# Context keys and values of the second block: kept in float32, the values computed in two halves at other places

## The chip, the cores and the metric

The kernel is one program on one core of a Trainium2 chip. The time is the device time of one execution in microseconds (us). TensorE (PE) multiplies, its weight loads are listed apart (PEld); VectorE is DVE, ScalarE is ACT, GpSimd is POOL, and SyncE (SP) issues nearly all transfers of weights from memory (HBM).

## The reference, cut to what matters

Two transformer blocks run one after the other on 256 tokens of width 1024. The first ends in a mixture of 32 experts; the second is a hybrid of a long convolution and an attention that also looks at a context of 256 tokens.

```python
# end of block one: each token goes to two of 32 experts
hb = jax.nn.silu(xb @ w1[e]) * (xb @ w3[e]);  out = hb @ w2[e]     # w1, w3: 1024x512, w2: 512x1024
x = rmsnorm(x + y, norm_f_g)
# block two: keys and values of the context do not depend on x
hc = modulate(rmsnorm_2(ctx, g_mix_pre), csh1, csc1)               # 256 x 1024
kv_c = hc @ w_in[:, OFF_K:OFF_G]                                   # 512 keys, 512 values; 1024 deep
h = modulate(rmsnorm_2(x, g_mix_pre), sh1, sc1);  proj = h @ w_in
k_all = concat([k, k_c]);  v_all = concat([v, v_c])                # used by the attention, late
```

## The kernel before, in words

All weights come through one queue, SP's, in tiles of 1 MB (128 partitions x 2048 float32). A ring of buffers (`wtile`, `wload`) gives each load the next slot, and SP issues a load when the slot's last reader is done; SP works in order, so a load whose slot is held stops those behind it.

A dense product in front of and behind the experts is exact to about float32 by splitting: each weight row block is split by ACT (`wh`, line 298) and DVE (`wl`, line 299) into a high and a low part of type fp32r, the other operand is split too (`cxh`, `cxl` for the context), and PE makes three products: high x high, low x high, high x low (`dense`, lines 310 to 312; `dense_T`, lines 346 to 348). The experts' products are single float32 products, read straight from the loaded tile (lines 1268 and 1298).

The stage that matters runs like this. After the cross attention of block one, x is transposed (line 268), scores for groups and experts are made (`lg`, line 852), and DVE finds each token's two experts in a chain of small operations that ends in `ea`; PE counts with it (`pp`, lines 906 to 910), DVE makes the one-hot rows (`hot`), and PE gathers the tokens of the first four experts (`pxg`, line 938). The context's keys (`ctx_k`, into `kTc`) and values (`ctx_v`, into `vc`) are written behind this in the code; the scheduler that builds the program places instructions of one engine by when their inputs are expected, so that they stand between the steps of the router.

Then come 16 cycles j of two experts each. A cycle is w1 (`up`, eight loads of 1 MB with w3), w2 of the cycle before (`down`, four loads), w3, the combination of the cycle before (`py`, line 1016), a gather for a later pair, in cycles 7 to 14 a piece of the second block's filters (`hooks`: `f1` to `fH`), and a transposition (`turn`). Two experts share PE, 64 columns each. The ring has 14 slots (4 `wpA`, 10 `wpB`); `change_ring` in `ctx_v` adds the two `xTB` buffers, which `cxh` and `cxl` held until then. In cycle 6 (`filters`) the ten `wpB` slots go and two `wpC` come, in cycle 15 (`wide_ring`) three more.

Behind the last combination stands a norm: ACT and DVE sum squares (`norm_part`), POOL takes the power, x is scaled (`xs`), PE transposes it (line 268), and ACT and DVE split it into `x2h` and `x2l`, into the same two `xTB` buffers, for the first products of block two.

Of the kernel before, what the change touches and what calls it, by code (L numbers as in the profile page):

```python
# [8 lines left out]
F32 = mybir.dt.float32  # L9
# [3 lines left out]
AF = mybir.ActivationFunctionType  # L13
# [4 lines left out]
P = 128  # L18
D = 1024
S = 256  # L20
# [81 lines left out]
def _body(nc, tc, I, out, ctx, dbg):  # L102
    V, A, G, T = nc.vector, nc.scalar, nc.gpsimd, nc.tensor

    traced = []
# [13 lines left out]
    def acc(name="acc"):  # L119
        return ps.tile([P, 512], F32, name=name, tag="acc", bufs=4)  # L120
# [7 lines left out]
    def xTt(name, g="A", dt=F32R, shape=(P, 8, S)):  # L128
        return wk.tile(list(shape), dt, name=name, tag="xT" + g, bufs=2)
# [4 lines left out]
    def tap(name, ap):  # L134
        if name in dbg:
            nc.gpsimd.dma_start(dbg[name], ap)
# [8 lines left out]
    def change_ring(new, gone=()):  # L145

        i = ring["i"] % len(ring["slots"])
        set_ring([pl for pl in ring["slots"][i:] + ring["slots"][:i] if pl not in gone] + new)
# [16 lines left out]
    def wloads(wsrc, c0, n, KB=8):  # L165
        return [wload(wsrc[kb * P:(kb + min(4, KB - kb)) * P, c0:c0 + n], min(4, KB - kb), n) for kb in range(0, KB, 4)]
# [104 lines left out]
    def tr_split(src, KB, gcol=None, sc=1.0, bcol=None, hl=None, name="t", g="A"):  # L271

        hi, lo = hl if hl else (xTt(name + "h", g), xTt(name + "l", g))
        for kk in range(0, KB, 2):
            pv = tr4(src, kk)
            if gcol is None:
                hilo(hi[:, kk:kk + 2, :], lo[:, kk:kk + 2, :], pv, sc)
                continue
            for j in range(2):
                k = kk + j  # L280
                if bcol is None:
                    hilo(hi[:, k, :], lo[:, k, :], pv[:, j, :], gcol[:, k:k + 1])
                else:
                    last["hi"] = A.activation(hi[:, k, :], pv[:, j, :], AF.Identity, bias=bcol[:, k:k + 1],  # L284
                                              scale=gcol[:, k:k + 1])
                    lo_of(lo[:, k, :], hi[:, k, :], pv[:, j, :], gcol[:, k:k + 1], bcol[:, k:k + 1])
        return hi, lo
# [14 lines left out]
    def dense(xh, xl, KB, ws, n, consume, ahead=None, tail=0):  # L302


        accs = [acc(), acc()]

        def products(k, t, h, l):
            s = slice(t * P, (t + 1) * P)
            p = accs[t][:, :n]
            T.matmul(p, xh[:, k, s], h[:, :n], start=k == 0, stop=False)  # L310
            T.matmul(p, xh[:, k, s], l[:, :n], start=False, stop=False)  # L311
            T.matmul(p, xl[:, k, s], h[:, :n], start=False, stop=k == KB - 1)  # L312
        held = []
        for k in range(KB):
            if ahead:
                ahead(k)
            held.append((k, split(ws[k // 4][:, k % 4, :], n)))
            if pend:
                pend.pop(0)()
            if k < KB - tail:  # L320
                for t in range(2):
                    products(k, t, *held[-1][1])
                held.pop()
            if k % 4 == 3 and after:
                after.pop(0)()
        for t in range(2):
            for k, hl in held:
                products(k, t, *hl)
            consume(t, accs[t][:, :n])

    def dense_T(xh, xl, KB, ws, n, consume, ahead=None):


        nb = n // P
        accs = [acc().rearrange("p (b s) -> p b s", b=2) for _ in range(0, nb, 2)]
        for k in range(KB):
            if ahead:
                ahead(k)
            h, l = split(ws[k // 4][:, k % 4, :], n)
            if pend:  # L340
                pend.pop(0)()
            for b in range(nb):
                s = slice(b * P, (b + 1) * P)
                p = accs[b // 2][:, b % 2, :]

                T.matmul(p, h[:, s], xh[:, k, :], start=k == 0 and b % 2 == 0, stop=False)  # L346
                T.matmul(p, h[:, s], xl[:, k, :], start=False, stop=False)  # L347
                T.matmul(p, l[:, s], xh[:, k, :], start=False, stop=k == KB - 1 and b in (nb - 1, b // 2 * 2 + 1))  # L348
            if k % 4 == 3 and after:
                after.pop(0)()  # L350
        for i, p in enumerate(accs):
            consume(i, p[:, :min(2, nb - 2 * i), :])
# [42 lines left out]
    def copy_to(dst, **kw):  # L395
        def c(t, p):
            A.activation(dst[:, t, :], p, AF.Copy, **{k: v[:, t:t + 1] for k, v in kw.items()})
        return c
# [277 lines left out]
    for g in range(8):  # L676
        p = smp("pmix")
# [121 lines left out]
    softmax(0)  # L799
    softmax(1)  # L800
    wxo = [wloads(I["w_xo"][0], ch * 512, 512) for ch in range(2)]
    wck = [wloads(I["w_in_2"][0], 2048 + ch * 512, 512) for ch in range(2)]
    for ch in range(2, 4):
        dense(mh, ml_, 8, W["w_xkv", ch], 512, copy_to(vx[:, :, (ch - 2) * 512:(ch - 1) * 512], scale=rm))
    oh, ol = xTt("oh", "A"), xTt("ol", "A")
# [11 lines left out]
    rc = rsq(sumsq(cx), 2, 1.0 / D)  # L817
    for t in range(2):
        V.tensor_scalar(cx[:, t, :], cx[:, t, :], rc[:, t:t + 1], None, op0=OP.mult)
    ch_, cl_ = tr_split(cx, 8, mods[:, 1, :], bcol=mods[:, 6, :], name="cx", g="B")  # L820
    for ch in range(2):
        dense(oh, ol, 8, wxo[ch], 512, add_x(ch))
    tap("x2", x)
# [129 lines left out]
    V.tensor_copy(pre_, p[:, :96].rearrange("p (c n) -> p c n", c=3))  # L953


    def ctx_k():
        def c_kc(i_, p):
            A.activation(kTc[:, 2 * i_:2 * i_ + 2, :], p, AF.Copy)
        dense_T(ch_, cl_, 8, wck[0], 512, c_kc)

    def ctx_v():
        dense(ch_, cl_, 8, wck[1], 512, copy_to(vc))
        change_ring(["xTB"] * 2)
    ctx_k()
    ctx_v()


    ge = mo.tile([P, 2, 4], F32, name="ge")
# [147 lines left out]
    def lambdas():  # L1116
        V.tensor_tensor(lv[:, 0:2, :], lv[:, 0:2, :], lv[:, 2:4, :], op=OP.mult)
        ls = mo.tile([1, 2], F32, name="ls")
        V.tensor_reduce(ls, lv[:, 0:2, :], AX.X, OP.add)
        A.activation(ls, ls, AF.Exp)  # L1120
        V.scalar_tensor_tensor(ls[:, 0:1], ls[:, 0:1], 0.2, ls[:, 1:2], op0=OP.add, op1=OP.subtract)
        p = smp("lam")
        traced[:] = [T.matmul(p[:, 0:1], ones[0:1, :], ls[:, 0:1], start=True, stop=True)]
        V.tensor_copy(lam, p[:, 0:1])
# [151 lines left out]
    def turn(sg):  # L1276
        p = tpp()
        for q in range(4):
            traced[:] = [T.transpose(p[:, q * P:(q + 1) * P], sg[:, q * P:(q + 1) * P], ident)]
        hT = wk.tile([P, 4, P], F32, name="hT", tag="wl", bufs=4)  # L1280
        A.activation(hT, p.rearrange("p (q s) -> p q s", q=4), AF.Copy)  # L1281
        return hT
# [19 lines left out]
    def gather_some(n):  # L1302
        for _ in range(min(n, len(todo))):
            todo.pop(0)()
# [14 lines left out]
    def after_down(j, po, done=None):  # L1319
        with pe_after():  # L1320
            combine(rows[:, 0], slotc[:, j:j + 1], po, done)
    for j in range(NJ):
        if j == 2:
            with pe_after():
                po = down(1, hT)
            with pe_after():
                gather_some(2)
            after_down(1, po)
            hT = None
            traced.clear()  # L1330
            overflow(n_over)
            traced.clear()
        if j % 2 == 0 and j + 2 < NJ:
            xg_, st_ = group(j + 2)
            xgs[j + 2] = xgs[j + 3] = xg_
            todo += st_
        h1 = acc("hw1")
        with pe_after():
            up(j, "w1", h1, (0, 1))
        sg = act_half(h1)  # L1340
        if j in (6, 15):
            hooks[j]()
        po = None
        if hT is not None:
            with pe_after():
                po = down(j - 1, hT)
        h3 = acc("hw3")
        with pe_after():
            up(j, "w3", h3, (0, 1))
        V.tensor_tensor(by_row(sg, 4), by_row(sg, 4), in_block(h3, 4), op=OP.mult)  # L1350
        if j == 0:
            lambdas()
            n_over = nc.values_load(novi[0:1, 0:1], min_val=0, max_val=7)
            with pe_after():
                bc_rows(rows[:, 0], dest)
                bc_rows(rows[:, 1], gt)
        if po is not None:
            after_down(j - 1, po)
        with pe_after():
            gather_some(4)  # L1360
        if 6 < j < 15 and j in hooks:
            with pe_after():
                hooks[j]()
        with pe_after():
            hT = turn(sg)
    with pe_after():
        po = down(NJ - 1, hT)
    after_down(NJ - 1, po, norm_part)
    tap("x3", x)
    moctx.close()  # L1370

# [18 lines left out]
    with tc.issue_after(last["hi"].ins):  # L1390
        for t in range(2):
            A.activation(x[:, t, :], xr[:, t, :], AF.Copy, scale=r1[:, t:t + 1])
    tap("xp", x)
    late["wc"].close()
    set_ring([wpA] * NA)
# [293 lines left out]
```

## Time and profile before

| | |
|---|---|
| median of 3 runs | 1294.23 us (1293.45 to 1294.81) |
| profiled execution | 1296.29 us, span 1294.6 us |
| PE busy | 1240.6 us (96%) |
| DVE, ACT, POOL busy | 747.9, 552.5, 70.2 us |
| read from HBM | 363.00 MB, 281 GB/s over the span |
| first and last expert product begin (line 1268) | 388.43 us, 838 us |

The page cuts the span into 40 slices of 32.4 us; slices 13 to 26 are the experts. Matmul rows are records: a float32 product appears as two, an fp32r product as one; their ends are modelled, and successive ones overlap, so the distance of two starts is the cost of one.

### The profile page before, as it was taken

What the parts mean: (1) busy time and instruction counts of PE and PEld (TensorE: products, weight loads), DVE (VectorE), ACT (ScalarE), POOL (GpSimd) and SP (SyncE); (2) the same over time, 40 slices, a digit from 0 to 9 for tenths busy, and PEclk for the clock granted to TensorE, in tenths of its full rate; (3) what the DMA queues carried; (4) which work ended last, traced back from release to release, by engine and by line L of the source; (5) the groups of instructions that cost most, each with busy time, mean ns of one, the idle gap of its engine ahead of it and who ended that gap; (6) DMA issues with size and microseconds to landing.
All of it is one profiled execution on the core that took longest, in us unless ns stands there. A gap on an engine that the chain in (4) does not pass through costs nothing.

```text
span 1294.6 us, 18193 instructions
## 1 busy us (share of the span) xinstructions
PE 1240.6 (96%) x6920; PEld 897.6 (69%) x6920; DVE 747.9 (58%) x1474; ACT 552.5 (43%) x1016; POOL 70.2 (5%) x118
## 2 busy tenths in 40 slices
PE   7999999999999999989899999979999998999996
PEld 7987788998884444433344444449878996799985
DVE  5996888746761413213341332369897787566654
ACT  6867455746551111111111111156255556445542
POOL 1101100100000000100000000010000101000000
PEclk9999999999999999999999999979999999999999
DMA  9764774994439999999999999967362666565751
GB/s 348 259 210 157 267 238 155 391 383 155 155 125 405 419 419 421 403 420 420 421 405 403 421 421 414 417 260 255 117 207 103 232 159 250 189 226 171 240 180 48
DMA packets 103243, 365.29 MB, mean 282 GB/s; under 512 B 6840, under 2 KB 9203, under 8 KB 78960
## 3 DMA queue, kind: packets, MB, share of 16 engines
q1 hardware_dynamic: 93264, 329.77, 67.6%
q0 software_dynamic: 9744, 34.18, 7.6%
q8 instruction: 56, 0.92, 0.3%
q14 instruction: 35, 0.29, 0.1%
q10 hardware_dynamic: 144, 0.14, 0.1%
HBM read 363.00 MB, written 1.06 MB: 281 GB/s over the span
## 4 chain that ended last, share of the span: by engine, by line
PE 50%; DMA 9%; issue 3%; DVE 2%; ACT 1%; POOL 1%; SPq 0%; DVEq 0%; POOLq 0%; ACTq 0%
PE hw L1268 13%; DMA w<-in_w_dram 7%; PE acc L347 5%; PE acc L346 5%; PE acc L348 5%; PE po L1298 3%; PE acc L312 2%; PE acc L311 2%; PE acc L310 2%; PE py L1016 2%; PE pxg L938 1%; PE iy L1454 1%; PE fH L1207 1%; PE s L1496 1%; DMA w<-in_w_ffn_gate_dram 1%
## 5 line engine op out<-in xcount | busy, mean ns | idle before, releaser
L298 ACT ACTIVATE wh<-w 128x512 fp32r<-128x512 f32 (+1 forms) x454 | 278.8, 622 | 242.7 <-PE acc L312 105.4
L299 DVE TENSOR_TENSOR wl<-w,wh 128x512 fp32r<-128x512 f32 (+1 forms) x454 | 303.5, 683 | 134.1 <-ACT wh L298 131.6
L1268 PE MATMUL hw<-w,xg 128*64 128x512 f32 x1024 | 234.8, 595 | 14.8 <-DMA w<-in_w_dram 12.9
L1268 PEld LDWEIGHTS hw<-w,xg 128*64 128x64 f32 x1024 | 79.3, 137 | 154.6 <-issue 127.2
L240 DVE SCALAR_TENSOR_TENSOR otl<-po,gs,oth 128x512 fp32r<-128x512 f32 x32 | 24.0, 749 | 208.7 <-ACT oth L239 207.9
L1298 PE MATMUL po<-w,hT 128*64 128x512 f32 x512 | 120.0, 595 | 2.2 <-ACT hT L1281 1.5
L1298 PEld LDWEIGHTS po<-w,hT 128*64 128x64 f32 x512 | 44.4, 137 | 72.1 <-issue 63.6
L939 ACT ACTIVATE xg<-pxg,vec 128x256 f32<-128x256 f32 x64 | 29.6, 476 | 139.3 <-PE pxg L938 139.0
L347 PE MATMUL acc<-xfl,wh 128*128 128x256 f32 x288 | 82.1, 285 | 0.0
L346 PE MATMUL acc<-xfh,wh 128*128 128x256 f32 x288 | 82.1, 285 | 0.0
L348 PE MATMUL acc<-xfh,wl 128*128 128x256 f32 x288 | 82.0, 285 | 0.0
L452 DVE SCALAR_TENSOR_TENSOR junk<-waT,cb 128x1024 bf16<-128x1024 f32 x64 | 78.1, 1220 | 3.6 <-DMA waT<-in_l_waT_dram 3.2
L311 PE MATMUL acc<-wl,xmh 128*128 128x512 f32 x192 | 76.7, 399 | 0.8 <-DVE wl L299 0.7
L312 PE MATMUL acc<-wh,xml 128*128 128x512 f32 x192 | 76.3, 398 | 0.0
L310 PE MATMUL acc<-wh,xmh 128*128 128x512 f32 x192 | 75.9, 399 | 0.0
L1350 DVE TENSOR_TENSOR sg<-sg,hw 128x512 f32<-128x512 f32 x16 | 11.0, 689 | 106.5 <-PE hw L1268 106.5
L239 ACT ACTIVATE oth<-po,gs 128x512 fp32r<-128x512 f32 x32 | 22.0, 687 | 101.2 <-PE po L1298 101.0
L347 PE MATMUL acc<-x2l,wh 128*128 128x256 f32 x224 | 64.3, 289 | 0.5 <-DVE x2l L246 0.5
L346 PE MATMUL acc<-x2h,wh 128*128 128x256 f32 x224 | 64.3, 292 | 0.3 <-ACT x2h L284 0.3
L348 PE MATMUL acc<-x2h,wl 128*128 128x256 f32 x224 | 64.4, 289 | 0.0
L347 PEld LDWEIGHTS acc<-xfl,wh 128*128 128x128 f32 x288 | 54.8, 190 | 0.0
L348 PEld LDWEIGHTS acc<-xfh,wl 128*128 128x128 f32 x288 | 54.8, 190 | 0.0
(542 smaller groups left out, 2568.8 us busy)
## 6 DMA issues: line engine op xcount, KB each, us to landing
w<-in_w_dram SPq DMA_DIRECT2D x188, 1024.0 KB, 13.6
w<-in_w_in_dram SPq DMA_DIRECT2D x54, 1024.0 KB, 6.3
waT<-in_l_waT_dram POOLq DMA_DIRECT2D x48, 512.0 KB, 5.3
w<-in_w_ffn_gate_dram SPq DMA_DIRECT2D x10, 1024.0 KB, 5.3
w<-in_w_ffn_up_dram SPq DMA_DIRECT2D x10, 1024.0 KB, 5.3
w<-in_w_ffn_down_dram SPq DMA_DIRECT2D x10, 1024.0 KB, 5.3
w<-in_w_out_dram SPq DMA_DIRECT2D x8, 1024.0 KB, 5.4
w<-in_w_xkv_dram SPq DMA_DIRECT2D x8, 1024.0 KB, 14.2
```

What stands on the lines that cost most here:

```text
L298: last["act"] = A.activation(h[:, :n], w, AF.Copy)
L299: last["dve"] = V.tensor_tensor(l[:, :n], w, f(h[:, :n]), op=OP.subtract)
L310: T.matmul(p, xh[:, k, s], h[:, :n], start=k == 0, stop=False)
L311: T.matmul(p, xh[:, k, s], l[:, :n], start=False, stop=False)
L312: T.matmul(p, xl[:, k, s], h[:, :n], start=False, stop=k == KB - 1)
L346: T.matmul(p, h[:, s], xh[:, k, :], start=k == 0 and b % 2 == 0, stop=False)
L347: T.matmul(p, h[:, s], xl[:, k, :], start=False, stop=False)
L348: T.matmul(p, l[:, s], xh[:, k, :], start=False, stop=k == KB - 1 and b in (nb - 1, b // 2 * 2 + 1))
L452: V.scalar_tensor_tensor(junk(), w[i_][:, b, :], 1.0, cb[:, r_, :], op0=OP.mult, op1=OP.mult, accum_out=adac[:, n, r_:r_ + 1])
L939: A.activation(xg[:, k, :], p, AF.Copy, scale=col["l_gmoe"][:, k:k + 1])
L1268: traced[:] = [T.matmul(hps[64 * e:64 * e + 64, :], xgs[j][:, 4 * kb + k, s0 + 64 * e:s0 + 64 * e + 64], we[e][:, k, :], start=kb + k == 0 ...
L1298: traced[:] = [T.matmul(po[hf][64 * e:64 * e + 64, :], hT[:, 2 * kb + q, 64 * e:64 * e + 64], we[e][:, q, hf * 512:(hf + 1) * 512], start= ...
```

## The change

The context stays in float32: transposed once (`cxT`), modulated by ACT, not split. Its keys are single float32 products, eight deep steps for four blocks of 128 keys, read from the unsplit weights. The values are made in two halves of 256 columns: the first half is loaded behind the weights of the first cycle and multiplied behind that cycle's gathers; the second half is loaded ahead of the last experts' w2 and multiplied behind the last combination. `cxT` takes one of the two `xTB` buffers until then, so the ring gets one, not two; the value weights are two loads of 1 MB in rows of 1 KB (before, two of 1 MB in rows of 2 KB, ahead of the experts).

```diff
-    wck = [wloads(I["w_in_2"][0], 2048 + ch * 512, 512) for ch in range(2)]
+    wck = wloads(I["w_in_2"][0], 2048, 512)
...
-    ch_, cl_ = tr_split(cx, 8, mods[:, 1, :], bcol=mods[:, 6, :], name="cx", g="B")
+    cxT = xTt("cxT", "B", F32)
+    for kk in range(0, 8, 2):
+        pv = tr4(cx, kk)
+        for j in range(2):
+            k = kk + j
+            A.activation(cxT[:, k, :], pv[:, j, :], AF.Identity, bias=mods[:, 6, k:k + 1], scale=mods[:, 1, k:k + 1])
+    change_ring(["xTB"])
...
-    def ctx_k():
-        def c_kc(i_, p):
-            A.activation(kTc[:, 2 * i_:2 * i_ + 2, :], p, AF.Copy)
-        dense_T(ch_, cl_, 8, wck[0], 512, c_kc)
-    def ctx_v():
-        dense(ch_, cl_, 8, wck[1], 512, copy_to(vc))
-        change_ring(["xTB"] * 2)
-    ctx_k()
-    ctx_v()
+    kc = [acc("kc") for _ in range(2)]
+    for k in range(8):
+        for b in range(4):
+            T.matmul(kc[b // 2][:, b % 2 * S:(b % 2 + 1) * S], wck[k // 4][:, k % 4, b * P:(b + 1) * P], cxT[:, k, :],
+                     start=k == 0 and b % 2 == 0, stop=k == 7 and b % 2 == 1)
+    for i_ in range(2):
+        A.activation(kTc[:, 2 * i_:2 * i_ + 2, :], kc[i_].rearrange("p (b s) -> p b s", b=2), AF.Copy)
+    def ctx_v(wv):
+        pv = [acc("cv")[:, :256] for _ in range(2)]
+        for k in range(8):
+            for t in range(2):
+                traced[:] = [T.matmul(pv[t], cxT[:, k, t * P:(t + 1) * P], wv[:, k, :], start=k == 0, stop=k == 7)]
+        return pv
+    def ctx_v_load(hf):
+        return wload(I["w_in_2"][0][:, 2560 + 256 * hf:2560 + 256 * (hf + 1)], 8, 256)
+    def ctx_v_out(hf, pv):
+        for t in range(2):
+            A.activation(vc[:, t, 256 * hf:256 * (hf + 1)], pv[t], AF.Copy)
...
             lambdas()
+            wv = ctx_v_load(0)
...
             gather_some(4)
+        if j == 0:
+            with pe_after():
+                ctx_v_out(0, ctx_v(wv))
...
+    wv = ctx_v_load(1)
     with pe_after():
         po = down(NJ - 1, hT)
     after_down(NJ - 1, po, norm_part)
+    with pe_after():
+        pv = ctx_v(wv)
...
             A.activation(x[:, t, :], xr[:, t, :], AF.Copy, scale=r1[:, t:t + 1])
+        ctx_v_out(1, pv)
```

On PE at the end of the router, before: the last products of the keys and values (`acc`), around the counts `pp`.

```order
L348 MATMUL acc<-cxh,wl 128x256
L310 MATMUL acc<-wh,cxh 128x512
L311 MATMUL acc<-wl,cxh 128x512
L312 MATMUL acc<-wh,cxl 128x512
L906 MATMUL pp<-ea,rt__3677 128x32
L907 MATMUL pp<-ea,rt__3677 128x32
L908 MATMUL pp<-ea,ca 128x32
L909 MATMUL pp<-ea,ca 128x32
L910 MATMUL pp<-ea,ca 128x32
L310 MATMUL acc<-wh,cxh 128x512
```

The same place after the change, from the last scores (`lg`) to the first gather; `kc` are the float32 keys.

```order
L858 MATMUL lg<-rt__3648,xmT 128x36 x9
L965 MATMUL kc<-cxT,w 128x256 x9
L912 MATMUL pp<-ea,rt__3648 128x32
L913 MATMUL pp<-ea,rt__3648 128x32
L914 MATMUL pp<-ea,ca 128x32
L915 MATMUL pp<-ea,ca 128x32
L916 MATMUL pp<-ea,ca 128x32
L965 MATMUL kc<-cxT,w 128x256 x7
L944 MATMUL pxg<-hot,xnh 128x256
```

Nine key products now stand ahead of `pp` and seven behind it; another seven stand behind the gathers, and the values are gone from here.

On SP's queue from the weights of the context to the first expert loads, before (`novi` is a number that SP reads to decide on a branch):

```order
L162 DMA w<-in_w_in_dram 128x4x512 x4
L1233 DMA w<-in_w_dram 128x2048 x13
L1353 TENSOR_LOAD novi
L1353 ISA x2
L1233 DMA w<-in_w_dram 128x2048 x19
```

And after:

```order
L162 DMA w<-in_w_in_dram 128x4x512 x2
L1251 DMA w<-in_w_dram 128x2048 x8
L162 DMA w<-in_w_in_dram 128x8x256
L1251 DMA w<-in_w_dram 128x2048 x5
L1372 TENSOR_LOAD novi
L1372 ISA x2
L1251 DMA w<-in_w_dram 128x2048 x20
```

The first half of the values (128x8x256) stands among the first expert loads; ahead of `novi` there are 13 expert loads in both.

On PE behind the last combination (`py`), after the change; before, the transposes `tp` followed `py` at once.

```order
L1034 MATMUL py<-oth,ET 128x512 x4
L1034 MATMUL py<-otl,ET 128x512 x4
L975 MATMUL cv<-w,cxT 128x256 x16
L268 MATMUL tp<-ca,xs_6783 128x128 x8
```

The 16 value products stand between the combination and the transposes.

## Rows read from the trace of the kernel before

**Rows 1.** The page's slices of 32.4 us: bytes moved.

```profile
GB/s 348 259 210 157 267 238 155 391 383 155 155 125 405 419 419 421 403 420 420 421 405 403 421 421 414 417 260 255 117 207 103 232 159 250 189 226 171 240 180 48
```

**Rows 2.** Stretches of the expert stage: us, busy (records) by engine, PEclk, DMA share, GB/s.

```profile
core 0: us, PE busy (x) PEld busy (x) DVE busy (x) ACT busy (x) POOL busy (x), PEclk, DMA share, GB/s
...
583.00:598.00 15.00, 11.83 (x53) 5.00 (x50) 4.02 (x7) 1.38 (x2) 0.00 (x0) 1.00 1.01 419
...
688.00:703.00 15.00, 15.00 (x80) 8.85 (x81) 2.96 (x5) 3.59 (x7) 0.00 (x0) 1.00 0.97 391
763.00:778.00 15.00, 14.72 (x66) 5.81 (x63) 3.12 (x9) 1.97 (x3) 0.00 (x0) 1.00 1.01 421
```

**Rows 3.** PE's timeline in the expert stage: start, us, what, [idle before, releaser].

```profile
388.43 13.95 PE L1268 MATMUL hw<-w,xg 128*64 128x512 f32 x64
...
407.10 7.09 PE L1268 MATMUL hw<-w,xg 128*64 128x512 f32 x32
...
551.54 2.79 PE L1298 MATMUL po<-w,hT 128*64 128x512 f32 x10 [0.60 <-DMA w<-in_w_dram]
...
774.59 3.65 PE L1268 MATMUL hw<-w,xg 128*64 128x512 f32 x14 [0.28 <-DMA w<-in_w_dram]
```

**Rows 4.** Groups by line: one of the keys' three product groups, busy, mean ns.

```profile
L346 PE MATMUL acc<-cxh,wh 128*128 128x256 f32 x32 | 9.4, 293 | 0.0
```

**Rows 5.** PE's timeline: float32 products, then fp32r products of keys and of values.

```profile
322.79 7.07 PE L810 MATMUL po<-pT,vx 128*128 128x256 f32 x32
...
369.90 0.28 PE L346 MATMUL acc<-cxh,wh 128*128 128x256 f32 x1
370.02 0.28 PE L347 MATMUL acc<-cxl,wh 128*128 128x256 f32 x1
...
386.07 0.39 PE L312 MATMUL acc<-wh,cxl 128*128 128x512 f32 x1
386.30 0.39 PE L310 MATMUL acc<-wh,cxh 128*128 128x512 f32 x1
```

**Rows 6.** Timelines of DVE and PE through the router.

```profile
365.37 0.42 DVE L867 SCALAR_TENSOR_TENSOR lg<-lg,rxm,brt 128x36 f32<-128x36 f32 x2
...
366.49 0.70 DVE L299 TENSOR_TENSOR wl<-w,wh 128x512 fp32r<-128x512 f32 x1
...
372.61 0.23 DVE L904 TENSOR_TENSOR ea<-E 128x64 f32<-128x64 f32 x1
...
372.89 0.41 PE L906 MATMUL pp<-ea,rt__3677 128*128 128x32 f32 x2
```

**Rows 7.** SP's timeline: issues of expert loads, start of the first, until the last.

```profile
384.62 4.55 SPq L1233 DMA_DIRECT2D w<-in_w_dram  x3
...
392.11 7.67 SPq L1233 DMA_DIRECT2D w<-in_w_dram  x6
...
682.84 5.30 SPq L1233 DMA_DIRECT2D w<-in_w_dram  x3
...
701.02 4.24 SPq L1233 DMA_DIRECT2D w<-in_w_dram  x4
```

**Rows 8.** Loads by line, 280 to 480 us, then the last w2 loads.

```profile
DMA to landing us min/median/max: 5.0/12.5/19.9
...
L1294 SPq DMA_DIRECT2D w<-in_w_dram x8: 328/328/422, 824.2 to 834.9; - x8
...
DMA to landing us min/median/max: 11.5/13.3/15.5
```

**Rows 9.** PE's timeline at the end of the experts.

```profile
842.75 7.09 PE L1298 MATMUL po<-w,hT 128*64 128x512 f32 x32 [0.75 <-ACT hT L1281]
...
859.93 1.99 PE L268 MATMUL tp<-ca,xs 128*128 128x128 f32 x8 [7.65 <-DVE xs L1387]
```

**Rows 10.** Stretches around the norm, columns as in rows 2.

```profile
844.00:848.00 4.00, 4.00 (x22) 1.33 (x20) 0.00 (x0) 0.00 (x0) 0.00 (x0) 1.00 1.04 389
...
864.00:868.00 4.00, 4.00 (x21) 4.00 (x21) 3.24 (x7) 2.69 (x6) 0.00 (x0) 0.50 1.01 398
...
872.00:880.00 8.00, 8.00 (x68) 7.99 (x68) 6.56 (x15) 5.86 (x9) 0.53 (x1) 1.00 0.52 195
```

## The prediction

> **What bounds the kernel now.** I read the bytes per slice first: slices 13 to 26 take some 400 to 421 GB/s, the ones around them far less [rows 1]. That is the expert stage, 32 experts of 6 MB each, all through SP's queue. Then the stage in stretches of 15 us: at 583:598 the DMA share is 1.01 at 419 GB/s while PE is busy for 11.83 of 15 us; at 763:778 PE has 14.72 and the DMA is still at 1.01 [rows 2]. PE's timeline says how it gets there. It starts the experts at 388.43 with its slots full, so for six cycles it runs at its own pace; the first wait on a load ends at 551.54, and the last, of 0.28 us, at 774.59 [rows 3]. So the stream of loads sets the middle of the stage, and PE and stream are level at its end. What counts is therefore not when PE starts the experts but when the stream starts, how much it still has to bring, and whether it ever runs out of free slots. At 421 GB/s a load of 1 MB takes 2.5 us.
>
> **1. The context products ahead of the experts (gain).** Removed on PE: 96 products of 256 columns for the keys (three groups of 32) [rows 4] and, by the same code, 3 x 16 of 512 columns for the values. Start to start they take 0.12 and 0.23 us [rows 5]: 96 x 0.12 + 48 x 0.23 = 22.5 us. Added there: the keys alone, 8 x 4 float32 products of 256 columns. The 16 products of that shape at line 810 are 32 records in 7.07 us with the tail of the last [rows 5], 0.43 us a product from start to start; 32 x 0.43 = 13.8 us. Net -8.7 us.
>
> What it loses is cover. In the new order nine key products stand between the router's scores and the counts (pp), seven between these and the gathers. DVE takes up the scores at 365.37 and begins ea, which pp waits for, at 372.61; between them stand seven splits wl like the one at 366.49, which push the next step back by 0.6 us each [rows 6]. They go: 4.2 us. On ACT one norm of x now stands ahead of two xmT copies, which I put at 0.5 us later scores. So pp can start at 372.89 - 4.2 + 0.5 = 369.2; PE, with nine products of 0.43 us behind the score products, which end when DVE takes them up (365.9), is there at 369.8. Behind pp the one-hot rows lose two splits and come at about 374.2, PE's seven products end at 374.0. With a wait for the first xmT copies I take 1.1 us of waits in all; the bounds are 0 and 4.2 us (no split's time comes back). **The experts start at 388.43 - 8.7 + 1.1 = 380.8**, 7.6 us earlier.
>
> **2. The stream of loads (takes most of it back).** Before, 13 loads are there and three more are issued from 384.62 to 389.2: the 14th, and two into the xTB buffers, freed when the context values end; pairs follow from 392.11 [rows 7]. A load into an empty queue lands 5.0 us after issue [rows 8], 2.5 of it transfer. So the 15th starts at about 388.8 + 2.5 = 391.3, load k lands at 391.3 + 2.5(k - 14), the 24th at 416.3.
>
> After, the ring has one xTB buffer (the other holds cxT to the end of the stage), and one of its 15 slots holds the first half of the value weights. At 380.8 there are again 13 expert loads, and the 14th is issued then, into the slot of the second key weights; it lands at 385.8. The next slots come back in pairs from 380.8 + 3.7 = 384.5 on (3.7 as from 388.43 to 392.11), four pairs until w3 ends at 380.8 + 14.0 = 394.8 [rows 3]. The first of them starts at 387, and the 22nd load has landed by 407. Before, PE was back at weights 4.7 us after the end of w3 (402.4 to 407.10). Now 16 value products stand there as well, 16 x 0.43 = 6.9 us: the value slot is free at about 405.9 and the first pair behind it at 410. The 23rd load lands at 410.9, the 24th at 415. The queue runs empty for 1.4 and 1.6 us. **The stream is 1.3 us ahead of before, not 7.6**: two loads fewer in store (5.0 us) and the gaps. PE itself is 7.6 - 6.9 = 0.7 us ahead and meets the stream where it did.
>
> **3. One slot fewer until the end (loses).** From the seventh cycle on the ring has 8 slots before and 7 after. The longest stretch without a release runs from the last issue of the three at 682.84 (688.1) to 701.02, 12.9 us [rows 7]. The pair ahead of it was in use for 4.0 us, and a new load needs 2.5 us to start: what is queued must last 19.4 us. 8 x 2.5 = 20 us does, 7 x 2.5 = 17.5 us falls 1.9 us short. Even with eight, that stretch has a share of 0.97 [rows 2]. Six cycles carry hooks of this kind, half of them as long as this one: 3 x 1.9 = 5.7 us at most, and 0 if loads that PE has not reached cover the gaps. I take 1.0, nearer to none, because PE waits little there [rows 3].
>
> **4. The second value load.** It stands in SP's queue ahead of the last eight half loads of w2. Those are issued until 834.9 and the last lands at least 11.5 us later, at 846.4 [rows 8]; PE needs it for the last quarter of the 7.09 us from 842.75, at 848.1 [rows 9]: a slack of 1.7 us. Where rows of 2 KB and 4 KB share the queue, it moves 389 GB/s [rows 10], and 1 MB takes 2.7 us; rows of 1 KB are in no row of a full queue, so 2.7 is the nearest. 2.7 - 1.7 = 1.0; the bounds are 0 (the stream has gained on PE by then) and 2.7.
> [...]
>
> **Expert stage: -1.3 + 1.0 + 1.0 = +0.7 us.**
>
> **5. The second half under the norm (free).** PE idles for 7.65 us ahead of the transposes at 859.93 [rows 9]; 6.9 us fit with 0.7 to spare, and the two copies out of PSUM stand on ACT behind the last split of x2. If that cover is gone, what exceeds it is paid in full.
>
> **6. The clock (gain).** [...]
>
> **Sum.** +0.7 - 1.5 = -0.8 us on the profiled execution's 1296.29 us, 1295.5. That execution took 2.1 us more than the median of the runs, so the median comes to 1294.2 - 0.8 = **1293.4 us**. The splits that go on ACT and DVE lie beside a full PE and bring nothing of their own.
>
> **Rivals.**
> - *The lead is kept* (28%). The queue does not run empty in the first cycle and w2 is not late: -4.3 for step 2, 0 for steps 3 and 4, -2.5 for the clock: 1294.2 - 6.8 = 1287.4. For it: PE waits for no load before 551. Against: every slot behind the value products comes back 6.9 us late.
> - *Seven slots starve the stream* (22%), slower. Step 3 in full, the clock at -1.0: -1.3 + 5.7 + 1.0 - 1.0 = +4.4, 1298.6. It decides where a stretch without a release passes 17.5 - 4.0 - 2.5 = 11.0 us. For it: the 0.97 with eight slots. Against: PE and stream are level there, so part of a gap is never waited for.
> - *The router's wait takes the products' place* (8%): waits of 4.2 rather than 1.1 us shift the stream by 3.1: 1296.5.
>
> **How the numbers follow.** The forecast has 42%, its own range is 1291.5 to 1295.5. No change means within 0.2%, 2.6 us, about what a measurement of this kernel can tell. Faster: nearly all of the first rival and a little of the forecast, 0.31. Slower: most of the second, half of the third, a little of the forecast, 0.26. Same: 0.43. A range that leaves out 2 in 10 goes from 1287.5 to 1298.5.
>
> **What would show it.** The first expert product near 381, not 388 us (step 1; later than 383 is the third rival). GB/s that dip between 404 and 413 us, and a first wait on a load within 3 us of before's (step 2; no dip is the first rival). DMA shares under 0.97 where the hooks are long (step 3). PE busy from the last py to the transposes, and a granted clock of 1.00 behind them (steps 5 and 6). The prediction is wrong if the last combination ends more than 3 us earlier or later than before.

## The result, and the profile after

The changed kernel took 1303.88 us (median of 4 runs, 1303.70 to 1305.19) against 1294.49 us (4 runs): a ratio of 1.0079, 95% interval 1.0064 to 1.0094. It is 9.4 us slower, and 1303.88 lies outside the predicted range, 1287.5 to 1298.5. Its profiled execution took 1303.7 us, span 1302.0 us.

The page's bytes per slice, to be laid beside [rows 1]:

```profile
GB/s 345 256 209 164 257 246 154 392 372 162 174 123 381 372 413 420 410 399 420 422 398 390 411 409 387 404 311 254 172 178 115 199 200 216 208 225 187 239 178 48
```

The stream loses mainly at three places: 381 for 405 in the 13th slice (391 to 423 us here), with the value half of the first cycle; 372 for 419 in the 14th, with the branch around the overflow code; and 398, 390, 411, 409, 387 and 404 in the 21st to 26th, the last third of the experts, where [rows 1] has 405, 403, 421, 421, 414 and 417.

PE's timeline (start, us, what, [idle before, releaser]), to be laid beside [rows 3] and [rows 9]:

```profile
380.74 13.95 PE L1286 MATMUL hw<-w,xg 128*64 128x512 f32 x64
398.87 7.07 PE L975 MATMUL cv<-w,cxT 128*128 128x256 f32 x32
...
448.31 16.46 PE L1286 MATMUL hw<-w,xg 128*64 128x512 f32 x64 [6.20 <-PEq L1049]
...
565.25 5.34 PE L1286 MATMUL hw<-w,xg 128*64 128x512 f32 x14 [3.26 <-DMA w<-in_w_dram]
...
815.02 3.65 PE L1286 MATMUL hw<-w,xg 128*64 128x512 f32 x14 [1.43 <-DMA w<-in_w_dram]
...
853.56 7.39 PE L1316 MATMUL po<-w,hT 128*64 128x512 f32 x32 [0.75 <-ACT hT L1299]
861.51 1.31 PE L1034 MATMUL py<-oth,ET 128*128 128x512 f32 x4 [0.56 <-ACT oth L239]
863.58 7.07 PE L975 MATMUL cv<-w,cxT 128*128 128x256 f32 x32
871.53 1.22 PE L268 MATMUL tp<-ca,xs 128*128 128x128 f32 x8 [0.88 <-DVE xs L1413]
873.35 0.50 PE L346 MATMUL acc<-x2h,wh 128*128 128x256 f32 x2 [0.60 <-ACT x2h L284]
...
880.60 0.63 PE L268 MATMUL tp<-ca,xs 128*128 128x128 f32 x4 [1.13 <-DVE tb L245]
```

The experts start 7.7 us earlier than before, and the last w2 product starts 10.8 us later (853.56 for 842.75). The first loss is in plain sight: PE idles for 6.20 us in front of cycle 2, and its sequencer (PEq) at line 1049, the branch around the overflow code, is named as the releaser. Waits for loads go on to 815.02, where before the last, of 0.28 us, was at 774.59.

Line 1049 of the changed kernel and the same line of the kernel before (1031): durations in ns (min/median/max), start in us. SP, ACT and DVE pass in 45 to 72 ns in both; PE does not:

```profile
L1049 SPq COMPARE_BRANCH  x1: 50/50/50, 424.6 to 424.6; - x1
L1049 ACTq COMPARE_BRANCH  x1: 45/45/45, 440.4 to 440.4; - x1
L1049 PEldq COMPARE_BRANCH  x1: 6065/6065/6065, 441.9 to 441.9; - x1
L1049 DVEq COMPARE_BRANCH  x1: 72/72/72, 442.8 to 442.8; - x1
```

```profile
L1031 PEldq COMPARE_BRANCH  x1: 445/445/445, 442.7 to 442.7; - x1
```

The transfers fit a wait for instructions. Queue 8 carries instructions, 55 packets and 0.90 MB in the whole execution, which is 16 KB for every 251 of the 13,808 records of PE and PEld: it follows PE. From 20 to 434 us of the kernel before, 18 packets move beside 4613 records, 256 a packet. The last of these packets ahead of the branch's end moves at 434 to 436 us before, some 7 us ahead of the branch, and at 444 to 446 us after, behind the branch's start (before first; packets, MB, share):

```profile
q8 instruction: 1, 0.02, 3.4%
```

```profile
q8 instruction: 1, 0.02, 3.5%
```

Windows of the changed kernel (us, busy and records by engine, PEclk, DMA share, GB/s) show what the stall sets off: behind it PE runs in part at a granted clock of 0.50 (448 to 452 us; the 64 records take 16.46 for 13.95 us), its slots come back late, and the stream has a hole, 146 GB/s at 450 to 455.

```profile
450.00:455.00 5.00, 5.00 (x18) 1.67 (x16) 1.90 (x7) 0.00 (x0) 0.00 (x0) 0.66 0.37 146
690.00:840.00 150.00, 145.49 (x668) 67.99 (x666) 37.08 (x74) 24.52 (x44) 0.00 (x0) 1.00 0.98 400
```

The second row, to be laid beside this one of the kernel before, is the other loss: 15 GB/s over 150 us are 2.25 MB or 5.3 us of the stream.

```profile
690.00:840.00 150.00, 149.43 (x697) 70.37 (x696) 39.05 (x81) 25.89 (x46) 0.54 (x1) 1.00 1.01 415
```

### The profile page after: what moved, and what is told of

Its sections match the earlier page's. It is cut to its first block, busy times and chain, and to the rows that moved or that the text cites. A ratio compares the mean times of both kernels' runs of the same rounds, so it can differ in the third digit from the quotient of the medians.

```text
span 1302.0 us, 18103 instructions
## 1 busy us (share of the span) xinstructions
PE 1244.6 (96%) x6904; PEld 897.2 (69%) x6904; DVE 731.9 (56%) x1442; ACT 542.6 (42%) x1002; POOL 70.0 (5%) x118
## 3 DMA queue, kind: packets, MB, share of 16 engines
HBM read 363.00 MB, written 1.06 MB: 280 GB/s over the span
## 4 chain that ended last, share of the span: by engine, by line
PE 52%; DMA 8%; DVE 2%; ACT 2%; issue 1%; POOL 0%; DVEq 0%; POOLq 0%; ACTq 0%
PE hw L1286 13%; DMA w<-in_w_dram 7%; PE acc L347 5%; PE acc L346 5%; PE acc L348 5%; PE po L1316 5%; PE acc L312 2%; PE acc L310 2%; PE acc L311 2%; PE py L1034 2%; PE pxg L944 1%; PE iy L1481 1%; PE fH L1225 1%; PE s L1523 1%; DMA w<-in_w_ffn_gate_dram 1%
## 5 line engine op out<-in xcount | busy, mean ns | idle before, releaser
L299 DVE TENSOR_TENSOR wl<-w,wh 128x512 fp32r<-128x512 f32 (+1 forms) x438 | 292.4, 682 | 134.9 <-ACT wh L298 133.9
L298 ACT ACTIVATE wh<-w 128x512 fp32r<-128x512 f32 (+1 forms) x438 | 268.9, 622 | 230.1 <-PE acc L312 102.3
L1286 PE MATMUL hw<-w,xg 128*64 128x512 f32 x1024 | 241.5, 604 | 23.2 <-DMA w<-in_w_dram 17.0
L1316 PE MATMUL po<-w,hT 128*64 128x512 f32 x512 | 116.2, 594 | 1.5 <-ACT hT L1299 1.5
```

The costliest lines, as they stand in the source:

```text
L298: last["act"] = A.activation(h[:, :n], w, AF.Copy)
L299: last["dve"] = V.tensor_tensor(l[:, :n], w, f(h[:, :n]), op=OP.subtract)
L1286: traced[:] = [T.matmul(hps[64 * e:64 * e + 64, :], xgs[j][:, 4 * kb + k, s0 + 64 * e:s0 + 64 * e + 64], we[e][:, k, :], start=kb + k == 0 ...
L1316: traced[:] = [T.matmul(po[hf][64 * e:64 * e + 64, :], hT[:, 2 * kb + q, 64 * e:64 * e + 64], we[e][:, q, hf * 512:(hf + 1) * 512], start= ...
```

## The experiments

Two theories on the branch. P: the code behind it lies in a block of instructions that was not yet fetched when PE arrived. Q: SP, whose queue has one more load in front of the same branch, is late, and all engines meet there. Two on the waits after 690. S: seven slots are too few. L: the stream was merely late from the hole on. "Last w2" is the start of the last w2 products, the clearest mark of the stage's end; GB/s is the window 690 to 840.

| run | time, us | against before, 95% interval | branch, ns | last w2 | slots | GB/s |
|---|---|---|---|---|---|---|
| before | 1294.49 | | 445 | 842.75 | 8 | 415 |
| changed | 1303.88 | 1.0064 to 1.0094 | 6065 | 853.56 | 7 | 400 |
| e1 page moved | 1300.53 | 1.0040 to 1.0086 | 445 | 847.61 | 7 | 395 |
| e2 page, before | 1296.54 | 1.0011 to 1.0038 | 6225 | 846.06 | 8 | 417 |
| e3 seven slots | 1301.16 | 1.0042 to 1.0081 | 458 | 852.70 | 7 | 390 |
| e4 half in cycle 7 | 1297.80 | 1.0027 to 1.0057 | 445 | 846.77 | 7 | 399 |
| c1 early, slot back | 1293.51 | 0.9993 to 1.0018 | 445 | 843.28 | 8 | 416 |
| c2 early, seven | 1297.74 | 1.0024 to 1.0059 | 442 | 849.07 | 7 | 404 |
| c3 key half late | 1299.37 | 1.0039 to 1.0077 | 445 | 848.84 | 8 | 416 |
| d1 later start | 1299.01 | 1.0029 to 1.0057 | 458 | 850.29 | 8 | 413 |
| c4 shrink +1 | 1293.42 | 0.9990 to 1.0013 | 445 | 843.68 | 8 | 417 |
| c5 shrink +2 | 1298.45 | 1.0026 to 1.0060 | 445 | 848.62 | 8 | 405 |
| f1 changed again | 1302.54 | 1.0059 to 1.0093 | 5926 | 852.08 | 7 | 399 |
| f2 e1 again | 1300.53 | 1.0041 to 1.0078 | 445 | 849.30 | 7 | 393 |

The kernel before ran beside each group, at medians of 1293.1 to 1294.3. The marks and windows come from one trace for each run: the two traces of the changed kernel (f1 is the second) differ by 1.5 us at the last w2 product, those of e1 and f2, one kernel too, by 1.7.

**e1, e2: the branch moved within its block.** The edit puts tiny products ahead of all of PE's work, in its first wait of 7.4 us: 24 in the changed kernel, 41 in the kernel before.

```diff
     G.memset(nhalf, -0.5)
+    pad = tpp("pad")
+    for _ in range(24):
+        T.matmul(pad[0:8, 0:8], nhalf, nhalf, start=True, stop=True)
```

> The changed kernel with 24 products of 8x8 (a few columns each) ahead of everything on TensorE, in its first wait of 7.4 us; nothing else moves, but each TensorE instruction after them stands 96 places later, so that the branch around the overflow code stands 3 places behind where the kernel before has it, and not 93 ahead of it. Theory P (the branch's target lies in a page of instructions that was not yet fetched; the 6.07 us of the branch on TensorE are that fetch): the branch takes under 1 us (0.445 before), the first w1 product of cycle 2 starts at 442 to 445 (448.31 in the changed kernel), the clock stays full there, the loads have no hole at 450 to 457. Rival Q (SyncE reaches the branch late, since one more load stands ahead of it and one slot is gone, and all engines meet there): the branch still takes 6 us and the time stays at 1303.9. What P is worth in the end tells two further theories apart. S (seven slots): the four waits for loads at 720 to 815 stay (4.4 us), 1297 to 1300. L (the stream was only late from the hole on): they go too, 1292.5 to 1295.5.

> The kernel before with 41 such products ahead of everything on TensorE: its branch now stands where the changed kernel's does within a block of 256 instructions. Theory P: the branch takes 4 to 7 us (0.445), 1298.5 to 1301.5. Rival Q: the branch is not touched, 1294.5 within 0.7.

The branch on PE, e1 first, then e2:

```profile
L1052 PEldq COMPARE_BRANCH  x1: 445/445/445, 440.6 to 440.6; - x1
```

```profile
L1034 PEldq COMPARE_BRANCH  x1: 6225/6225/6225, 443.0 to 443.0; - x1
```

P holds both ways and Q falls: the stall leaves the changed kernel and appears in the kernel before, with SP's queue untouched. The packet of queue 8 goes the same way: in e1 it moves at 432 to 434 us, ahead of the branch, in e2 at 446 to 448, behind the branch's start. In e1 the first w1 product of cycle 2 starts at 442.64, the granted clock of 372 to 520 is 1.00 (0.98 in the changed kernel), and the first wait for a load ends at 551.94, where [rows 3] has 551.54. Of the time, less than expected: in e2 the late branch costs 3.3 us at the last w2 product and some 3 us of the time (1.0024), since PE would have waited for loads from 551 on anyway. In e1 the four waits after 690 stay (1.19, 1.31, 1.33, 1.12 us), which speaks for S; and e2, late by the same stall but with eight slots, has one wait of 0.64 us there and 417 GB/s, which speaks against L.

**f1, f2: the size of the branch in the changed kernel, both on one chip.** f1 is the changed kernel, f2 is e1 once more.

> The changed kernel as it is, on the same chip as the next one, to size the branch in it by time and not by one trace: 6 to 7 us on TensorE at the branch, 1.0064 to 1.0094 of the kernel before.

> The changed kernel with 24 tiny products ahead, once more. If the branch costs what the last w2 product shows (847.61 against 853.56), 4 to 6.5 us faster than the changed kernel on this chip; if the later waits for loads take half of it back, as in the kernel before with the late branch (3.3 of 6.4), 2 to 4.

2.0 us by the medians, 2.8 us at the last w2 product. The first pair of traces had 5.95, but there 1.3 us stood ahead of the branch, since e1 starts its experts at 379.44; f1 and f2 start theirs at 380.11 and 380.14. So the second half of the expectation: the stall is partly taken back by later waits. The traces show it, the transposition `tp` at the end of cycle 2 being 6.4 us later in f1 (465.64 for 459.24) and that of cycle 15 2.8 us (850.68 for 847.90). The single times overlap (1301.3 to 1304.96 against 1298.85 to 1303.06), so that the 2.0 us are uncertain by about as much.

**e3: only the slot.**

```diff
-        change_ring(["xTB"] * 2)
+        change_ring(["xTB"])
```

> The kernel before with one ring slot fewer from the experts on (the second of the two 8 KB buffers is simply not given to the ring): 15 and then 7 slots, as in the changed kernel, everything else as before. Theory S (the seven slots cost the last third of the stage): waits for loads after 690 in most cycles, about one us each, 1298 to 1299.5. Theory L, which is the step of the prediction (one slot fewer costs 1.0 us, at most 5.7): no more than one such wait after 690, 1294.5 to 1296.

The kernel before, with nothing but one slot fewer, is as slow as the changed kernel without its stall: 8.0 us, and more than either theory had. Its window 690 to 840 (columns as above), and PE's waits for loads at 690 to 850:

```profile
690.00:840.00 150.00, 145.70 (x666) 67.06 (x666) 37.11 (x74) 24.50 (x44) 0.00 (x0) 1.00 0.96 390
```

```profile
PE hw L1268 <- DMA w<-in_w_dram: 4.1, 3, 1.4
```

Up to 660 the slot costs nothing that can be seen: 411 GB/s at 520 to 580 as before. From there on it does, ahead of 690 too: at 660 to 680 (before first) the stream has 371 GB/s for 396, PE's wait for a load at 685.44 is 2.83 us where the one at 684.13 was 1.32, and the granted clock of 680 to 690 is 0.84.

```profile
660.00:680.00 20.00, 19.63 (x83) 7.49 (x84) 9.92 (x21) 3.16 (x6) 0.53 (x1) 1.00 1.01 396
```

```profile
660.00:680.00 20.00, 19.21 (x83) 7.31 (x83) 10.05 (x23) 2.57 (x4) 0.53 (x1) 1.00 0.97 371
```

```profile
685.44 5.34 PE L1268 MATMUL hw<-w,xg 128*64 128x512 f32 x14 [2.83 <-DMA w<-in_w_dram]
```

The whole loss can be read from the transposition `tp` at the end of cycle 9 to that of cycle 15, before first: 177.4 us against 188.1.

```profile
664.00 0.60 PE L1279 MATMUL tp<-ca,sg 128*128 128x128 f32 x4
...
841.35 0.66 PE L1279 MATMUL tp<-ca,sg 128*128 128x128 f32 x4 [0.60 <-DVE x L1018]
```

```profile
663.19 0.60 PE L1279 MATMUL tp<-ca,sg 128*128 128x128 f32 x4
...
851.30 0.66 PE L1279 MATMUL tp<-ca,sg 128*128 128x128 f32 x4 [0.59 <-DVE x L1018]
```

The same stretch takes 183.4 to 188.1 us in every trace with seven slots, and 176.8 to 178.6 in those with eight, but for c5, where pieces of the filters stand in pairs (182.2).

**c1, c2: the slot in the changed arrangement.** Both halves go into cycles 3 and 4, where the ring has its 15 slots; c1 gives the context's buffer to the ring behind them, c2 does not (it lacks the last two lines).

```diff
-        if j == 0:
+        if j in (3, 4):
+            wv = ctx_v_load(j - 3)
             with pe_after():
-                ctx_v_out(0, ctx_v(wv))
+                ctx_v_out(j - 3, ctx_v(wv))
+            if j == 4:
+                change_ring(["xTB"])
```

> The changed kernel with both value halves in the expert cycles 3 and 4 (15 slots, and TensorE not yet waiting for loads), nothing under the norm, and the context's buffer given to the ring after cycle 4, so that there are 8 slots and not 7 from cycle 6 on; 40 tiny products ahead keep the branch where it is fast. Theory S (the eighth slot carries the last third): after 690 no more waits for loads than in the kernel before. If the stream of loads sets the pace up to 684, the two products (13.8 us) are taken up by TensorE's waits for loads there (12.9 us in the kernel before) and the last w2 product starts at 840 to 843 (842.75 before): 1290 to 1293.5. If TensorE sets it, the 13.8 us stand in full against the 7.7 us of the earlier start: 1297 to 1300.

> The same without giving the slot back: 7 slots. Theory S: waits of about one us in most cycles after 690, and 4 to 9 us slower than the run with the slot given back. Theory L (lateness, not slots, made the waits of the changed kernel): within 1 us of it.

S again: 4.2 us by the medians, 5.8 us at the last w2 product. After 690 c1 waits for loads once, 0.42 us (before 0.22 and 0.28), c2 four times, 0.78 to 1.16 us. The window 690 to 840 of c1, then of c2, and 20 us of c2 in which the stream's share falls to 0.91:

```profile
690.00:840.00 150.00, 149.50 (x698) 71.20 (x697) 39.02 (x82) 25.88 (x46) 0.54 (x1) 1.00 1.01 416
```

```profile
780.00:800.00 20.00, 20.00 (x100) 10.51 (x100) 3.15 (x5) 4.19 (x8) 0.00 (x0) 1.00 0.91 366
...
690.00:840.00 150.00, 147.00 (x681) 69.46 (x679) 38.47 (x80) 25.90 (x46) 0.54 (x1) 1.00 0.99 404
```

c1 is level with the kernel before, at the slow end of what was expected where the stream sets the pace (843.28 for 840 to 843, 1293.51 for 1290 to 1293.5). Its 13.8 us of products in the cycles cost nothing, as expected, but the earlier start brings nothing either.

**e4, c3: other places.** In e4 the first half stands in cycle 7, the second under the norm; in c3 (with the slot given back) one half of the keys stands in cycle 5.

> The changed kernel with the instructions moved as in the run with 24 products (here 40, since the 16 context products are no longer ahead of the branch), and the first half of the values, its load and its 6.9 us of products, in cycle 7, where TensorE waits for loads anyway, and not in cycle 0. If what sets the end of the experts is the stream of loads, and the products in cycle 0 stop it for 3 us (357 GB/s at 400 to 420): 2 to 4 us faster than the run with 24 products. If TensorE sets it: the same within 0.7, since the same work is only moved. If the stop only moves along to cycle 7: the same, with a hole in the loads there.

> The run with the slot given back, and of the keys too only one half ahead of the experts; the other half (one load of 1 MB, 6.9 us of products) in cycle 5, the slot given back after it. If the stream sets the pace, the experts start at 373 to 375 and not at 380.8, the stream of loads with them, and 3 to 6 us are saved against that run: 1285 to 1289. If the router's chain takes the place of the products ahead of the experts, or TensorE sets the pace: the same as that run within 1.5.

e4 is 2.7 us faster than e1 by the medians, at intervals that overlap. c3 missed: the first w1 product starts at 377.75, not at 373 to 375 (the gathers now wait 2.50 us for `hot`), and the half in cycle 5, just ahead of the smaller ring, stops the stream, 270 GB/s at 540 to 560:

```profile
540.00:560.00 20.00, 20.00 (x97) 11.09 (x97) 4.74 (x14) 2.87 (x5) 3.79 (x7) 1.00 0.73 270
```

**d1, c4, c5: where the earlier start of c1 went.** My theory G was that the stream's lead is lost where the ring shrinks. d1 delays the experts of the kernel before by 16 idle products; c4 and c5 shrink c1's ring one and two cycles later.

```diff
     ctx_v()
+    pd = acc("pd")
+    for _ in range(16):
+        T.matmul(pd[:, 0:256], ident, kTc[:, 0, :], start=True, stop=True)
```

```diff
-    hooks = {0: lambdas, 6: filters, 15: wide_ring}
+    hooks = {0: lambdas, 7: filters, 15: wide_ring}
```

> The kernel before with 16 idle float32 products of 128x256 (6.9 us by the row of such products) between the context values and the first expert, so that the experts start 6.9 us later; 48 tiny products ahead keep the branch at its place within a block of 256. Theory G (what the stream of loads is ahead is given back where the ring shrinks from 16 to 8 slots, at cycle 6): the kernel before has 1.75 MB or 4.3 us to give back there (133.1 MB at 540 instead of 134.9), so that only 1 to 3.5 us of the 6.9 are left at the last w2 product. Rival K (the lead is kept, as the prediction's second case has it): 6 to 7 us are left.

> The run with the halves in cycles 3 and 4 and the slot given back, but the ring shrinks in cycle 7 and not 6 (the filter's code, which needs the room, starts one cycle later and its first two pieces stand in one cycle). Theory G: TensorE catches up on the loads by some 2.4 us a cycle, so that less is given back: 1 to 3 us faster than that run, with 36 to 39 MB moved at 540 to 640 where it moved 38.0 at 520 to 620. If what the loads are ahead does not matter: the same within 0.7.

> The same with the shrink in cycle 8 and four of the filter's pieces in pairs. Theory G: 2 to 5 us faster than the run with the shrink in cycle 6, unless the paired pieces (the same work in six cycles and not eight) stop the stream where 8 slots are left: then no faster than with the shrink in cycle 7.

G falls as an account of the kernel before. d1's experts start at 396.13, 7.7 us late, and its last w2 products are 7.5 us late, 5.4 us by the medians (the profiled execution was 4.1 us above its median): most of a shift of the stream is carried to the end. It speaks against L as well: late with eight slots, d1 has one wait of 0.18 us behind that at 690.96 (684.13 before). c4 gains nothing over c1, and c5 loses, with 337 GB/s at 720 to 740 where pieces of the filters stand in pairs. What I had read as a stop in the kernel before is none: at 520 to 540 the engines are full at 398 GB/s, with POOL's loads for the filters among them.

```profile
520.00:540.00 20.00, 19.92 (x102) 10.32 (x100) 7.72 (x14) 4.60 (x8) 3.81 (x7) 1.00 1.03 398
```

So where did the 8.4 us of c1's earlier start go (379.98 for 388.43)? Both kernels read 363.00 MB in all, so that the bytes moved up to a time show the lead, the two value loads (5.0 us of the stream) that c1 still has to bring included: 114.04 MB at 440 us against 113.11, 0.9 MB or 2 us. The prediction's step 2 had 1.3 us for the changed kernel. These 2 us go in cycle 6, where the ring shrinks: at 540 to 560 c1's stream (first) has 340 GB/s for 413, and by 560 it has moved 162.32 MB against 162.91.

```profile
540.00:560.00 20.00, 19.92 (x98) 8.47 (x97) 9.18 (x25) 5.53 (x9) 3.79 (x7) 1.00 0.92 340
```

```profile
540.00:560.00 20.00, 18.05 (x74) 5.90 (x68) 5.06 (x18) 1.97 (x3) 0.00 (x0) 1.00 1.01 413
```

c4, which shrinks the ring a cycle later, is still 0.9 MB ahead at 560 (163.83) and 0.8 MB behind at 660 (204.16 against 204.99): the later shrink only moved the loss. What it is made of stays open. No version that I ran beats the kernel before by more than the measurement can tell.

## Why the prediction was wrong, point by point

**Step 1 was right.** First expert product at 380.74 (380.8), pp at 369.59 (369.2), waits of 0.82 and 0.38 us in the router (1.1).

**Step 2 was right in what it counted and missed what stood next to it.** PE is back at weights at 406.31, 0.8 us ahead of before (0.7). The dip came where it was put: 277 GB/s at 404 to 413 us, before (second) 420.

```profile
404.00:413.00 9.00, 9.00 (x45) 4.20 (x46) 0.00 (x0) 1.37 (x3) 0.00 (x0) 1.00 0.79 277
```

```profile
404.00:413.00 9.00, 9.00 (x55) 4.90 (x55) 3.26 (x10) 2.34 (x5) 0.00 (x0) 1.00 1.01 420
```

By 420 us the changed kernel had moved 104.04 MB against 104.74, with the second value load, 1.05 MB, still to come, which the prediction counts in step 4; so its expert loads were 0.35 MB or 0.8 us ahead (1.3). In the changed kernel itself the first wait for a load ends at 565.25, 13.7 us later than before; with the stall taken out (e1) it ends 0.4 us from before's. The mark I had named was 3 us. c1, whose value loads also stand in the stage, and whose slot is back, ends the stage within 0.6 us of before. What failed is the sentence "PE itself is 0.7 us ahead and meets the stream where it did": it took PE's work in cycles 0 to 5 as unchanged. The change takes 93 records out of PE's order ahead of the branch at line 1049, and so, as e1 and e2 show, the branch's target fell into a block that was not there (its packet of queue 8 moved at 444 to 446 us, behind the branch's start at 441.9): 6.2 us instead of 1.85 us in front of cycle 2, and 2.5 us more for the 64 records behind it (16.46 for 13.95), in part at a clock of 0.50. It cost 2.0 us of the time (f1 against f2) to 3.4 us (the first runs of the changed kernel against e1), either uncertain by some 2 us. The branch's 445 ns stood in the trace of before, and I did not ask what they depend on.

The branch took 5.9 to 6.2 us where it stalled (f1, the changed kernel, e2), in the changed kernel beside the expert stream at 417 GB/s (440 to 448 us). How much of it the stream makes, no run shows.

**Step 3 failed by its size.** The term "one slot fewer" was +1.0 us with 5.7 as its bound. It measured 4.2 us by time in the changed arrangement (c2 against c1) and 8.0 us in the kernel before (e3). The bound counted three long stretches without a release; in e3's trace every cycle from 10 on is longer than before, by 0.6 to 3.8 us. "Nearer to none, because PE waits little there" was the error. PE waited little there because eight slots just sufficed, as I read the balance at 763:778 in [rows 2]: a full stream (1.01) beside a full PE (14.72 of 15 us) left no slack on either side, and what the stream lost in e3 (390 GB/s for 415) PE waited for, 4.1 us at 690 to 850. The second rival, seven slots starve the stream, had this mechanism and 1298.6 us; e1 and f2, the changed kernel without the stall, took 1300.5. The stated range ended at 1298.5, just under that rival's own value, though the rival had 22%.

**Step 4 was right.** The last half loads come late behind the second value load: ACT's `oth` starts 7.2 us after the last w2 products begin, where it was 6.35 us before, 0.86 us (1.0). These products take 7.39 to 7.70 us in the five traces with the value load there, and 7.09 in the nine without it, e3 with its seven slots among them.

```profile
860.77 1.27 ACT L239 ACTIVATE oth<-po,gs 128x512 fp32r<-128x512 f32 x2 [7.26 <-PE po L1316]
```

**Step 5 was right.** The 7.07 us of value products end at 870.65, and PE still waits 0.88 us for xs.

**Step 6 was wrong in its worth.** The clock stays at 1.00 where [rows 10] has 0.50:

```profile
872.00:880.00 8.00, 6.18 (x47) 5.43 (x45) 6.29 (x14) 6.53 (x13) 2.57 (x5) 1.00 0.75 249
```

But nothing is gained: PE now waits for ACT and DVE (0.60 and 1.13 us in the timeline above, and 0.68 us between them). From the first transposition to the last weight load of line 346's first group it takes 41.0 us before (859.93 to 900.9), 40.8 after (871.53 to 912.3) and 40.5 in e3 (869.88 to 910.4), where the granted clock is 0.50 at 868 to 872 and 0.63 at 872 to 880. No run shows the 1.5 us that the sum takes off for the clock, an estimate from the records and clocks of [rows 10]: the stretch is 0.2 us shorter than before at a clock of 1.00, and 0 was the value to take.

```profile
L346 PEld LDWEIGHTS acc<-x2h,wh x96: 186/192/338, 862.3 to 900.9; 128*128 128x128 f32 x96
```

```profile
L346 PEld LDWEIGHTS acc<-x2h,wh x96: 187/192/192, 873.3 to 912.3; 128*128 128x128 f32 x96
```

```profile
L346 PEld LDWEIGHTS acc<-x2h,wh x96: 186/192/337, 872.2 to 910.4; 128*128 128x128 f32 x96
```

In sum: the prediction's -0.8, with nothing for the clock in place of -1.5, 2.0 to 3.4 for the branch, and 4.2 to 8.0 for the slot in place of 1.0, comes to 5.9 to 11.1 us slower; 9.4 was measured. The two do not add up exactly, since the stall hides in waits that the missing slot makes too.

## What to carry to other kernels

A buffer that a moved operation keeps is a part of the move: where the stream of loads and TensorE are level, one slot of eight was worth 4.2 us (c2 against c1) to 8.0 us (e3), more than all that the move saved. An early start pays only by what the bounding stream gains (2 of the 8.4 us in c1), and a load that moves from ahead of a full stream into it takes its whole transfer out of that gain (5.0 us for the two value loads there). Where the code has a branch, count the instructions in front of it in both versions: 93 records fewer made this one 6065 ns long instead of 445.

## What the runs showed of the hardware

The branch took 442 to 458 ns in the kernel before, in e1, e3, e4, c1 to c5, d1 and f2, and 5926 to 6225 ns in the changed kernel, f1 and e2. The stalled ones stand 93 records earlier in PE's order than the kernel before, or, in e2, 164 places later: 257 apart, 6065 and 6225 ns. d1, 257 records behind the kernel before, passes in 458 ns (445). Both fit the 256 records a packet of queue 8 above; whether other places stall, these runs do not show.

From the first transposition behind the norm to the end of the span, the same code took 434.67 us in the profiled execution of the kernel before, 430.47 in that of the changed kernel and 429.62 in e3. Some 3 of the 4.2 us between before and after arise at line 370. There the traces of before, c1, c4, d1 and e1 have PE wait 2.65 to 3.44 us for `xfl`, and their stretch takes 431.8 to 434.7 us; the other nine wait 1.08 to 2.01 us, and theirs takes 429.6 to 430.5. In those five the granted clock falls behind that wait, to 0.52 to 0.74 in the lowest window of 4 us; in the changed kernel, c2, e3, f1 and f2 it stays at 1.00. That is the larger part of why the spans differ by 7.4 us and the last w2 products by 10.8. It is no matter of the change: e1 and f2, one kernel, wait 3.17 and 2.01 us. What makes the wait longer is open. Before, then after:

```profile
PE acc L370 <- DVE xfl L246: 2.7, 1, 2.7
```

```profile
PE acc L370 <- DVE xfl L246: 1.2, 1, 1.2
```
